# Rotary embedding on one core: six rows of a tile in two groups of three, two rows through TensorE, and declared-away waits

## The chip, the cores and the metric

The kernel runs on one core of a Trainium2 chip. The metric is the device time of one execution in microseconds. The kernel before took 163.06 us, the median of 3 runs (162.94 to 163.31).

## What is computed

x has 16 batches, 512 positions and 1024 channels in float32. The channels of a position are 16 heads of 64. Each head is cut into two halves of 32, x1 and x2, which are rotated by the angle of the position; cos and sin are 512 x 32 and the same for every batch and head.

```python
x = x.reshape(batch, seq, num_heads, head_dim)
x1, x2 = (x[..., :half_dim].copy(), x[..., half_dim:].copy())
rotated = np.concatenate([x1 * cos - x2 * sin, x1 * sin + x2 * cos], axis=-1)
```

So each element needs two products and a sum: x times cos, plus the other half of the head times sin, with a minus for the first half. x is 33.5 MB and the output is 33.5 MB.

## The kernel before, in words

**Tiles.** A tile is two batches: 128 partitions, each with 8 consecutive positions ("rows") of 1024 elements, 32 KB a partition and 4 MB a tile. There are NT = 8 tiles and NB = 5 buffers for x; the result is written over x in the same buffer and stored from there. Tiles 5, 6 and 7 use the buffers of tiles 0, 1 and 2, so their loads wait for the stores of those tiles.

**Tables.** cos and sin lie on 64 partitions and are spread to 128 by products on TensorE with a selecting matrix (L93 to L95). sns holds, per row, -sin for the first half and sin for the second, so one product with it over a view that swaps the halves of each head (`swapped`) gives the second term. sns_ps and cos_ps are the same tables in PSUM; VectorE reads its tables from there, GpSimd reads sns in SBUF.

**Three paths for a row**, all in `compute`:

- Rows 2 to 7 go in PAIRS of two rows. GpSimd makes T = swapped(x) * sns (L131, two T buffers). VectorE makes pp = x * cos in PSUM (L147, one buffer) and then writes x = T + pp (L148).
- Row 0: GpSimd makes B = swapped(x) * sns (L126), VectorE multiplies x by cos in place (L136).
- Row 1: VectorE makes both (L126 and L136).
- For rows 0 and 1 TensorE adds the two in PSUM by products with the identity (L141 with x, L142 with B), in parts of 512 elements, and ScalarE copies each part back into x (L143). ps has two buffers there, one PSUM bank each.

**Order.** The order of the code on each engine is kept as written (`manual_schedule`); the layer below adds the waits that the data and the buffers need. In a tile VectorE does B of row 1, the in-place products of rows 1 and 0, then three times a product and a sum. GpSimd does B of row 0, then three T. A pool's new tile waits until the last reader of the buffer's old tile is done.

**Transfers.** SyncE issues all loads and stores of x and out on one queue, in program order, and waits at each until its condition holds: load 0 in four pieces, loads 1 to 4, stores 0 to 2, loads 5 to 7, stores 3 to 6, store 7 in four pieces. ScalarE issues the two loads of the tables. A store waits for VectorE's sums and for ScalarE's copies of the tile.

Of the kernel before, what the change touches and what calls it, by code (L numbers as in the profile page):

```python
# [7 lines left out]
FP32 = mybir.dt.float32  # L8
ALU = mybir.AluOpType


@with_exitstack
def kernel(
    ctx: ExitStack,
    tc: tile.TileContext,
    x: bass.AP,
    cos: bass.AP,
    sin: bass.AP,
    num_heads: bass.AP,
    out: bass.AP,  # L20
):
    nc = tc.nc
    P = nc.NUM_PARTITIONS
    batch, seq, dim = x.shape
    nh = num_heads
    hd = dim // nh
    half = hd // 2


    BP = 2  # L30
    HP = P // BP
    R = seq // HP
    NT = batch // BP
    assert HP * R == seq and BP * NT == batch
    NB = 5
    PAIRS = (2, 4, 6)
    PEROWS = (0, 1)

    xv = x.rearrange("b (p r) d -> (b p) (r d)", r=R)
    xv = xv.rearrange("(t p) f -> t p f", p=P)  # L40
    ov = out.rearrange("b (p r) h d -> (b p) (r h d)", r=R)
    ov = ov.rearrange("(t p) f -> t p f", p=P)
    cosv = cos.rearrange("(p r) j -> p (r j)", r=R)
    sinv = sin.rearrange("(p r) j -> p (r j)", r=R)

    fixed = ctx.enter_context(tc.tile_pool(name="fixed", bufs=1))
    xin = ctx.enter_context(tc.tile_pool(name="xin", bufs=NB))
    tpool = ctx.enter_context(tc.tile_pool(name="tpool", bufs=2))
    bpool = ctx.enter_context(tc.tile_pool(name="bpool", bufs=2))
    ptab = ctx.enter_context(tc.tile_pool(name="ptab", bufs=1, space=bass.MemoryType.PSUM))  # L50
    ppair = ctx.enter_context(tc.tile_pool(name="ppair", bufs=1, space=bass.MemoryType.PSUM))
    prow = ctx.enter_context(tc.tile_pool(name="prow", bufs=2, space=bass.MemoryType.PSUM))

    ctx.enter_context(tc.manual_schedule())


    x_tiles = [None] * NT
    Q = 2 * dim

    def load(t, pieces=1):  # L60
        x_tiles[t] = xin.tile([P, R * dim], FP32, name="x_sb")
        n = R * dim // pieces
        for i in range(pieces):
            nc.sync.dma_start(out=x_tiles[t][:, i * n:(i + 1) * n], in_=xv[t][:, i * n:(i + 1) * n])

    def store(t, pieces=1):
        n = R * dim // pieces
        for i in range(pieces):
            nc.sync.dma_start(out=ov[t][:, i * n:(i + 1) * n], in_=x_tiles[t][:, i * n:(i + 1) * n])

    load(0, pieces=4)
    tabs = fixed.tile([HP, 2, R * half], FP32, name="tabs")
    nc.scalar.dma_start(out=tabs[:, 1], in_=sinv)
    nc.scalar.dma_start(out=tabs[:, 0], in_=cosv)
    for t in range(1, NB):
        load(t)


    ident = fixed.tile([P, P], FP32, name="ident")
    nc.gpsimd.memset(ident, 0.0)  # L80
    nc.gpsimd.affine_select(  # L81
        out=ident, in_=ident, compare_op=ALU.not_equal, fill=1.0,
        base=0, pattern=[[-1, P]], channel_multiplier=1,
    )
    sel = fixed.tile([HP, 2, P], FP32, name="sel")
    nc.vector.tensor_copy(out=sel[:, 0, :HP], in_=ident[:HP, :HP])  # L86
    nc.vector.tensor_copy(out=sel[:, 0, HP:], in_=ident[:HP, :HP])
    nc.vector.tensor_scalar_mul(out=sel[:, 1, :], in0=sel[:, 0, :], scalar1=-1.0)

    sns_ps = ptab.tile([P, R, 2, half], FP32, name="sns_ps")  # L90
    cos_ps = ptab.tile([P, R, half], FP32, name="cos_ps")
    sin3 = tabs[:, 1].rearrange("p (r j) -> p r j", r=R)
    nc.tensor.matmul(out=sns_ps[:, :, 1, :], lhsT=sel[:, 0, :], rhs=sin3, start=True, stop=True)  # L93
    nc.tensor.matmul(out=sns_ps[:, :, 0, :], lhsT=sel[:, 1, :], rhs=sin3, start=True, stop=True)  # L94
    nc.tensor.matmul(out=cos_ps.rearrange("p r j -> p (r j)"), lhsT=sel[:, 0, :], rhs=tabs[:, 0],  # L95
                     start=True, stop=True)
    sns = fixed.tile([P, R, 2, half], FP32, name="sns")
    cost = fixed.tile([P, R, half], FP32, name="cost")
    nc.scalar.copy(out=sns, in_=sns_ps)  # L99
    nc.scalar.copy(out=cost, in_=cos_ps)  # L100

    def view(ap, r0, n):

        return ap[:, r0 * dim:(r0 + n) * dim]

    def cosb(tab, r0, n):
        return bass.AP(tensor=tab.tensor, offset=tab.offset + r0 * half,
                       ap=[tab.ap[0], [half, n], [0, 2 * nh], [1, half]])

    def snsb(tab, r0, n):  # L110
        return bass.AP(tensor=tab.tensor, offset=tab.offset + r0 * hd,
                       ap=[tab.ap[0], [hd, n], [0, nh], [1, hd]])

    def swapped(xt, r0, n):
        return bass.AP(tensor=xt.tensor, offset=xt.offset + r0 * dim + half,
                       ap=[xt.ap[0], [hd, n * nh], [-half, 2], [1, half]])

    def compute(t):
        xt = x_tiles[t]
        ts = {}  # L120
        bs = {}

        for r in PEROWS:
            B = bpool.tile([P, dim], FP32, name="B")
            eng = nc.vector if r == PEROWS[-1] else nc.gpsimd
            eng.tensor_tensor(out=B, in0=swapped(xt, r, 1), in1=snsb(sns_ps if eng is nc.vector else sns, r, 1),  # L126
                              op=ALU.mult)
            bs[r] = B
        for r0 in PAIRS:
            T = tpool.tile([P, 2 * dim], FP32, name="T")  # L130
            nc.gpsimd.tensor_tensor(out=T, in0=swapped(xt, r0, 2), in1=snsb(sns, r0, 2), op=ALU.mult)  # L131
            ts[r0] = T

        for r in reversed(PEROWS):
            xr = view(xt, r, 1)
            nc.vector.tensor_tensor(out=xr, in0=xr, in1=cosb(cos_ps, r, 1), op=ALU.mult)  # L136
            for c in range(2):
                ps = prow.tile([P, dim // 2], FP32, name="ps")
                xc = xr[:, c * dim // 2:(c + 1) * dim // 2]
                bc = bs[r][:, c * dim // 2:(c + 1) * dim // 2]  # L140
                nc.tensor.matmul(out=ps, lhsT=ident, rhs=xc, start=True, stop=False)  # L141
                nc.tensor.matmul(out=ps, lhsT=ident, rhs=bc, start=False, stop=True)  # L142
                nc.scalar.copy(out=xc, in_=ps)  # L143
        for r0 in PAIRS:
            pp = ppair.tile([P, 2 * dim], FP32, name="pp")
            xr = view(xt, r0, 2)
            nc.vector.tensor_tensor(out=pp, in0=xr, in1=cosb(cos_ps, r0, 2), op=ALU.mult)  # L147
            nc.vector.tensor_tensor(out=xr, in0=ts[r0], in1=pp, op=ALU.add)  # L148

    for t in range(NB):  # L150
        compute(t)
        if t < NT - NB:
            store(t)
    for t in range(NB, NT):
        load(t)
    for t in range(NT - NB, NB):
        store(t)
    for t in range(NB, NT):
        compute(t)
        store(t, pieces=4 if t == NT - 1 else 1)  # L160


# [33 lines left out]
```

## Time and profile before

One execution was taken by the profiler. Its own time is 162.99 us, its span 161.0 us: some 2 us lie around the span.

| what | value |
|---|---|
| runs, median (lowest to highest) | 163.06 us (162.94 to 163.31) |
| profiled execution, its span | 162.99 us, 161.0 us |
| mean granted TensorE clock | 0.758 |
| VectorE's first product, end of its last sum | 8.86 us, 150.60 us |
| a load or store of 4096 KB, issue to landing (median) | 29.5 us, 27.0 us |
| HBM read, written | 33.69 MB, 33.55 MB |

How to read a profile like this one: engines are PE (TensorE's products), PEld (its weight loads), DVE (VectorE), ACT (ScalarE), POOL (GpSimd) and SP (SyncE). A group of instructions is given as line, engine, operation, the tiles it writes and reads, shapes and count; then the busy time in us and the mean ns of one; then the idle time of the engine just before them and what ended it. L131 is line 131 of the kernel before. The rows of busy tenths and of the DMA cut the span into 40 equal slices; 9 is 90% or more. A row of a stretch gives its length, the busy us (and count) of each engine in it, the granted TensorE clock, the DMA share and the GB/s.

### The profile page before, as it was taken

How to read it: one execution, taken by the hardware profiler on the slowest of the kernel's cores; microseconds unless marked ns; L12 is line 12 of the kernel's file. 1: busy time of each engine (PE TensorE's matmuls, PEld its weight loads, DVE VectorE, ACT ScalarE, POOL GpSimd, SP SyncE). 2: the span in 40 equal slices, each digit the busy share in tenths (PEclk: the TensorE clock that was granted, in tenths of full speed). 3: DMA queues.
4: the chain of work that ended last, by engine and by line, in shares of the span. 5: the costliest groups of instructions: out<-in, count | busy, mean ns of one | idle time of the engine just before them, and what ended most of it. 6: DMA issues, size and time to landing. Idle time of an engine off the chain costs nothing. (4 is left out here: it accounts for less than half of the span.)

```text
span 161.0 us, 581 instructions
## 1 busy us (share of the span) xinstructions
PE 78.3 (49%) x134; PEld 32.3 (20%) x134; DVE 137.8 (86%) x75; ACT 21.0 (13%) x35; POOL 127.1 (79%) x38
## 2 busy tenths in 40 slices
PE   0449900598019910894049700990079803991000
PEld 0223300233014400341024200340034202340000
DVE  1077999999999999999999999999999999999400
ACT  3021210014001210022002300121001400121000
POOL 1079999999998799959995999869995999692000
PEclk9999996569755985589957995699655975598555
DMA  5999999999999999999999999999999999999994
GB/s 181 385 419 480 391 497 415 391 472 440 391 456 456 391 432 480 391 415 489 399 417 472 407 415 464 415 407 472 423 399 456 448 399 456 448 391 417 421 423 187
DMA packets 3329, 67.25 MB, mean 418 GB/s; under 512 B 384, under 2 KB 512, under 8 KB 512
## 3 DMA queue, kind: packets, MB, share of 16 engines
q1 hardware_dynamic: 3168, 67.11, 97.6%
q10 hardware_dynamic: 160, 0.13, 0.3%
q14 instruction: 1, 0.01, 0.0%
HBM read 33.69 MB, written 33.55 MB: 418 GB/s over the span
## 5 line engine op out<-in xcount | busy, mean ns | idle before, releaser
L131 POOL TENSOR_TENSOR T<-x_sb,sns 128x2048 f32<-128x2048 f32 x24 | 108.2, 4526 | 10.5 <-DVE x_sb L148 10.5
L141 PE MATMUL ps<-x_sb,ident 128*128 128x512 f32 x64 | 44.8, 790 | 61.0 <-issue 40.4
L148 DVE TENSOR_TENSOR x_sb<-T,pp 128x2048 f32<-128x2048 f32 x24 | 54.9, 2288 | 3.4 <-POOL T L131 1.0
L147 DVE TENSOR_TENSOR pp<-x_sb,cos_ps 128x2048 f32<-128x2048 f32 x24 | 55.0, 2294 | 0.6
L142 PE MATMUL ps<-B,ident 128*128 128x512 f32 x64 | 40.3, 717 | 0.0
L143 ACT COPY x_sb<-ps 128x512 f32<-128x512 f32 x32 | 18.8, 586 | 117.6 <-PE ps L142 117.6
L141 PEld LDWEIGHTS ps<-x_sb,ident 128*128 128x128 f32 x64 | 15.2, 253 | 83.3 <-issue 80.4
L126 POOL TENSOR_TENSOR B<-x_sb,sns 128x1024 f32<-128x1024 f32 x8 | 18.8, 2346 | 7.6 <-ACT sns L99 7.6
L142 PEld LDWEIGHTS ps<-B,ident 128*128 128x128 f32 x64 | 15.4, 241 | 22.0 <-issue 22.0
L136 DVE TENSOR_TENSOR x_sb<-x_sb,cos_ps 128x1024 f32<-128x1024 f32 x16 | 18.8, 1218 | 0.5
L126 DVE TENSOR_TENSOR B<-x_sb,sns_ps 128x1024 f32<-128x1024 f32 x8 | 9.7, 1217 | 7.0 <-ACT sns L99 7.0
L93 PE MATMUL sns_ps<-tabs,sel 64*128 64x256 f32 x2 | 1.2, 697 | 6.2 <-DMA tabs<-in_sin_dram 6.2
L93 PEld LDWEIGHTS sns_ps<-tabs,sel 64*128 64x128 f32 x2 | 0.5, 310 | 6.1 <-issue 6.1
L99 ACT ACT_TABLE_LOAD x1 | 1.3, 1283 | 1.9 <-issue 1.9
L86 DVE COPY sel<-ident 64x64 f32<-64x64 f32 x1 | 0.2, 185 | 1.3 <-POOL ident L81 1.3
L99 ACT COPY sns<-sns_ps 128x512 f32<-128x512 f32 x1 | 0.6, 586 | 5.0 <-PE sns_ps L94 5.0
L95 PE MATMUL cos_ps<-tabs,sel 64*128 64x256 f32 x2 | 1.2, 711 | 0.0
L94 PE MATMUL sns_ps<-tabs,sel 64*128 64x256 f32 x2 | 1.1, 631 | 0.0
L94 PEld LDWEIGHTS sns_ps<-tabs,sel 64*128 64x128 f32 x2 | 0.7, 334 | 0.2
L95 PEld LDWEIGHTS cos_ps<-tabs,sel 64*128 64x128 f32 x2 | 0.5, 306 | 0.6 <-DMA tabs<-in_cos_dram 0.6
L100 ACT COPY cost<-cos_ps 128x256 f32<-128x256 f32 x1 | 0.4, 373 | 0.5 <-PE cos_ps L95 0.5
L80 POOL MEMSET ident<- 128x128 f32 x1 | 0.2, 204 | 0.3 <-POOLq L177 0.3
(7 smaller groups left out, 1.1 us busy)
## 6 DMA issues: line engine op xcount, KB each, us to landing
x_sb<-in_x_dram SPq DMA_DIRECT2D x7, 4096.0 KB, 29.5
out_dram<-x_sb SPq DMA_DIRECT2D x7, 4096.0 KB, 27.0
x_sb<-in_x_dram SPq DMA_DIRECT2D x4, 1024.0 KB, 8.7
out_dram<-x_sb SPq DMA_DIRECT2D x4, 1024.0 KB, 9.2
tabs<-in_sin_dram ACTq DMA_DIRECT2D x1, 64.0 KB, 5.3
tabs<-in_cos_dram ACTq DMA_DIRECT2D x1, 64.0 KB, 6.7
```

What stands on the lines that cost most here:

```text
L93: nc.tensor.matmul(out=sns_ps[:, :, 1, :], lhsT=sel[:, 0, :], rhs=sin3, start=True, stop=True)
L94: nc.tensor.matmul(out=sns_ps[:, :, 0, :], lhsT=sel[:, 1, :], rhs=sin3, start=True, stop=True)
L95: nc.tensor.matmul(out=cos_ps.rearrange("p r j -> p (r j)"), lhsT=sel[:, 0, :], rhs=tabs[:, 0], start=True, stop=True)
L99: nc.scalar.copy(out=sns, in_=sns_ps)
L126: eng.tensor_tensor(out=B, in0=swapped(xt, r, 1), in1=snsb(sns_ps if eng is nc.vector else sns, r, 1), op=ALU.mult)
L131: nc.gpsimd.tensor_tensor(out=T, in0=swapped(xt, r0, 2), in1=snsb(sns, r0, 2), op=ALU.mult)
L136: nc.vector.tensor_tensor(out=xr, in0=xr, in1=cosb(cos_ps, r, 1), op=ALU.mult)
L141: nc.tensor.matmul(out=ps, lhsT=ident, rhs=xc, start=True, stop=False)
L142: nc.tensor.matmul(out=ps, lhsT=ident, rhs=bc, start=False, stop=True)
L143: nc.scalar.copy(out=xc, in_=ps)
L147: nc.vector.tensor_tensor(out=pp, in0=xr, in1=cosb(cos_ps, r0, 2), op=ALU.mult)
L148: nc.vector.tensor_tensor(out=xr, in0=ts[r0], in1=pp, op=ALU.add)
```

## The change

The change gives the 8 rows of a tile another split and writes out which waits are left to others.

- Rows 0 to 2 and 3 to 5 are two groups of three (G, GROUPS): one T, one pp and one sum each, of 3072 elements. Rows 6 and 7 (PEROW) go through TensorE together: one B of 2048 elements on GpSimd, one in-place product a on VectorE, four parts of 512.
- In tile 0 VectorE makes B itself, from sns in SBUF. VectorE has no B in the other tiles.
- PSUM: pp is 3072 elements, so ps has one buffer instead of two. sin's spread table uses ps too; cos_ps stays; sns_ps and the unused copy of cos are gone. sel is written by GpSimd, and ScalarE makes both halves of sns.
- GpSimd's order is T, T in tile 0; T, B, T in tiles 1, 2 and 5 (AFIRST); B, T, T in the others. VectorE begins a tile with a in tiles 1, 2, 5 and 7, and with pp in the others.
- `implied` drops the wait of an instruction for another that an earlier wait of its engine covers; `after` adds a wait. With `after`, VectorE's first product waits for GpSimd's first T in tile 0, a of tiles 3, 4 and 6 waits for the tile's first T, and the second T of tiles 2, 3, 5 and 6 waits for the next tile's load.
- Loads 0 and 1 and stores 5 and 7 are cut at other places.

```diff
-    PAIRS = (2, 4, 6)
-    PEROWS = (0, 1)
+    G = 3
+    GROUPS = (0, 3)
+    PEROW = 6
+    AFIRST = (1, 2, 5)
...
-    ppair = ctx.enter_context(tc.tile_pool(name="ppair", bufs=1, space=bass.MemoryType.PSUM))
-    prow = ctx.enter_context(tc.tile_pool(name="prow", bufs=2, space=bass.MemoryType.PSUM))
+    pgrp = ctx.enter_context(tc.tile_pool(name="pgrp", bufs=1, space=bass.MemoryType.PSUM))
+    prow = ctx.enter_context(tc.tile_pool(name="prow", bufs=1, space=bass.MemoryType.PSUM))
...
+    def implied(inst, *others):
+        for o in others:
+            tc.declare_no_dep(inst.ins, o.ins, reason="implied by an earlier wait of the engine")
...
-    load(0, pieces=4)
+    load(0, (0, 1, 2 * G, 2 * R))
...
+    load(1, (0, 2 * G, 2 * R))
...
-    nc.tensor.matmul(out=sns_ps[:, :, 1, :], lhsT=sel[:, 0, :], rhs=sin3, start=True, stop=True)
-    nc.tensor.matmul(out=sns_ps[:, :, 0, :], lhsT=sel[:, 1, :], rhs=sin3, start=True, stop=True)
+    nc.tensor.matmul(out=sin_ps, lhsT=sel, rhs=tabs[:, 1], start=True, stop=True)
...
-    nc.scalar.copy(out=sns, in_=sns_ps)
-    nc.scalar.copy(out=cost, in_=cos_ps)
+    nc.scalar.copy(out=sns[:, :, 1, :], in_=sin3)
+    nc.scalar.mul(out=sns[:, :, 0, :], in_=sin3, mul=-1.0)
...
+    def second(eng, pool, name, t, r0, n):
+        o = pool.tile([P, n * dim], FP32, name=name)
+        return o, eng.tensor_tensor(out=o, in0=swapped(x_tiles[t], r0, n), in1=snsb(r0, n), op=ALU.mult)
...
+    def pe_rows(t, a):
+        xr = view(x_tiles[t], PEROW, 2)
+        for c in range(4):
+            ps = prow.tile([P, dim // 2], FP32, name="ps")
+            xc = xr[:, c * H:(c + 1) * H]
+            nc.tensor.matmul(out=ps, lhsT=ident, rhs=xc, start=True, stop=False)
+            nc.tensor.matmul(out=ps, lhsT=ident, rhs=Bs[t][:, c * H:(c + 1) * H], start=False, stop=True)
+            i = nc.scalar.copy(out=xc, in_=ps)
...
+        if t == 0:
+            order = (0, 1)
+        elif t in AFIRST:
+            order = (0, "b", 1)
+        else:
+            order = ("b", 0, 1)
...
+        if t == 0:
+            pp, p1 = dve_p(t, 0)
+            after(p1, TIs[t, 0])
+            implied(p1, *loads[t])
+            implied(dve_s(t, 0, pp), *loads[t])
+            Bs[t], b = second(nc.vector, bpool, "B", t, PEROW, 2)
+            a = dve_a(t)
+            pp, p2 = dve_p(t, 1)
+            s2 = dve_s(t, 1, pp)
+        elif t in AFIRST or t == NT - 1:
+            a = dve_a(t)
+            pp, p1 = dve_p(t, 0)
+            s1 = dve_s(t, 0, pp)
+            q, p2 = dve_p(t, 1)
+            s2 = dve_s(t, 1, q)
...
+        else:
+            pp, p1 = dve_p(t, 0)
+            a = dve_a(t)
+            after(a, TIs[t, 0])
+            s1 = dve_s(t, 0, pp)
+            q, p2 = dve_p(t, 1)
+            s2 = dve_s(t, 1, q)
...
-        store(t, pieces=4 if t == NT - 1 else 1)
+        if t == NT - 1:
+            store(t, (0, 2 * G, 4 * G, 2 * R))
+        else:
+            store(t, (0, R, 2 * R) if t == NB else (0, 2 * R))
```

dve_p is pp = x * cos, dve_s the sum T + pp into x, dve_a the in-place product of rows 6 and 7; gp_b and gp_t call `second` on GpSimd. The second T of a tile carries the wait for the next tile's load through a list that is gone through at the end of the program. The instructions that VectorE's order of a tile holds are thus 5 in tiles 1 to 7 and 6 in tile 0.

## The prediction

> **What bounds the kernel now.** I read the table of busy times first, then the DMA row, then the groups of instructions, then the order in time of three tiles, and at last stretches of the span with the granted clock and the DMA rate in each.
>
> ```profile
> PE 78.3 (49%) x134; PEld 32.3 (20%) x134; DVE 137.8 (86%) x75; ACT 21.0 (13%) x35; POOL 127.1 (79%) x38
> ...
> DMA  5999999999999999999999999999999999999994
> ...
> q1 hardware_dynamic: 3168, 67.11, 97.6%
> ...
> L131 POOL TENSOR_TENSOR T<-x_sb,sns 128x2048 f32<-128x2048 f32 x24 | 108.2, 4526 | 10.5 <-DVE x_sb L148 10.5
> ...
> L148 DVE TENSOR_TENSOR x_sb<-T,pp 128x2048 f32<-128x2048 f32 x24 | 54.9, 2288 | 3.4 <-POOL T L131 1.0
> L147 DVE TENSOR_TENSOR pp<-x_sb,cos_ps 128x2048 f32<-128x2048 f32 x24 | 55.0, 2294 | 0.6
> ...
> L126 POOL TENSOR_TENSOR B<-x_sb,sns 128x1024 f32<-128x1024 f32 x8 | 18.8, 2346 | 7.6 <-ACT sns L99 7.6
> ...
> L136 DVE TENSOR_TENSOR x_sb<-x_sb,cos_ps 128x1024 f32<-128x1024 f32 x16 | 18.8, 1218 | 0.5
> ```
>
> The DMA row is full from the second slice to the last but one, and queue q1, which carries x and out, takes 97.6% of the span. VectorE (DVE) is almost as full: it works from 8.86 us to 150.60 with gaps of 0.03 to 0.11. So two chains run side by side, the byte stream and VectorE's loop of 17.55 us a tile (80.11 to 97.66 from B to B). GpSimd (POOL) has slack: 10.5 us of its time goes in waits for a sum to free a T buffer. The stretches show how full the stream is:
>
> ```profile
> 8.00:148.00 140.00, 76.43 (x131) 31.18 (x130) 134.76 (x71) 19.71 (x34) 126.35 (x32) 0.77 1.01 434
> 150.00:158.00 8.00, 0.00 (x0) 0.00 (x0) 0.60 (x1) 0.00 (x0) 0.00 (x0) 0.50 1.01 427
> 158.00:161.00 3.00, 0.00 (x0) 0.00 (x0) 0.00 (x0) 0.00 (x0) 0.00 (x0) 0.50 0.22 93
> ```
>
> The last two numbers of a row are the DMA share and GB/s. The stream moves 434 GB/s in the middle and 427 in the last store. After 158.00 only 0.28 MB moves, 0.65 us of the stream, so bytes end at 158.65 and the span 2.35 later. Since the stream is full, work taken from VectorE cannot bring much; work that comes later than the stream needs it costs its full delay. So I ask when each store becomes ready after the change.
>
> **The parts, with durations.** GpSimd's products run back to back 2.30 us for one row (40.43 to 42.73) and 4.495 for two (8.99 for a pair), so a row more costs 2.195 and three rows 6.69. GpSimd now makes two products of three rows and one of two in each tile: 2 x 6.69 + 4.50 = 17.88 us, where it had 2.30 + 3 x 4.495 = 15.8. VectorE: 1.218 for one row, 2.294 for two, so 1.076 a row and 3.37 for three, with 0.11 from product to sum and 0.03 from sum to product (53.22 + 2.30, next at 55.62; that ends 57.91, next at 57.94). A tile is 2.33 + 2 x 3.48 + 2 x 3.40 = 16.1 us instead of 17.55. **GpSimd becomes the longer of the two**, 17.9 against 16.1, and above the old 17.55.
>
> Waits left out: VectorE's gaps in the loop are 3.5 us in all (3.4 + 0.6 + 0.5 of idle time ahead of its three lines, less 1.0 of waiting for T). A shorter program can save at most that, on an engine that now waits for GpSimd; I cost it at nothing. The instruction queue moved one packet of 0.01 MB, so no fetch shows either.
>
> **Start.** The sin table lands and TensorE starts at 6.17; one product instead of two ends near 7.2 (the second began at 7.15); a copy of 256 elements takes 0.37 (that of cos_ps), the negated one I take alike; GpSimd starts at 8.2, not 8.91. The first three rows of x, 1.57 MB, are there: 2.26 MB had moved by 8.0. Loads and stores are cut elsewhere, but SyncE's queue issues 22 before and after: nothing. VectorE began at 8.86; now its first product waits for GpSimd's first T, 8.2 + 6.69 = 14.9. Behind it stands VectorE's whole program.
>
> **A clash that no row shows.** In tile 0 VectorE makes B from x and sns, both in SBUF; in every loop product and sum of the trace one of its inputs lies in PSUM. GpSimd's T of tile 1 becomes free at the same instant (both wait for the first sum, 21.8). If the two do not disturb each other, as one-SBUF rows do not (a sum is 2.29 beside GpSimd and 2.29 alone at 148.31), the cost is 0. If they exclude each other, either GpSimd waits for VectorE's 2.3 us or VectorE waits for GpSimd's 6.7. I take 2.3, the middle one: after a sum VectorE has started its next instruction at 53.22, 70.78, 88.34 and GpSimd at 53.27, 70.83, 88.39, so VectorE is first by 0.05.
>
> The Trainium skill, SBUF — State Buffer, section "Who interferes with whom", states that a VectorE instruction with two SBUF inputs contends with a GpSimd instruction that reads SBUF. By it the cost would be 2.3 or 6.7 and not 0. No row of this trace shows such a pair.
>
> **The two engines, walked forward.** End times in us; T(t,0) needs the first sum of tile t-1 (two T buffers), T(t,1) the second; a of tiles 1, 2, 5 stands first on VectorE and needs B, which GpSimd makes second there.
>
> | tile | GpSimd, in its order | VectorE a, first sum, second sum |
> |---|---|---|
> | 0 | T 14.9, T 21.6 | first sum 21.8, B 24.1, a 26.4, second 33.3 |
> | 1 | T 30.9, B 35.4, T 42.1 | 37.7, 44.6, 51.5 |
> | 2 | T 51.3, B 55.8, T 62.5 | 58.2, 65.1, 72.0 |
> | 3 | B 67.0, T 73.7, T 80.4 | 77.7, 81.1, 88.0 |
> | 4 | B 84.9, T 91.6, T 98.3 | 93.9, 97.3, 104.2 |
> | 5 | T 105.0, B 109.5, T 116.2 | 111.8, 118.7, 125.6 |
> | 6 | B 120.6, T 127.3, T 134.0 | 131.3, 134.7, 141.6 |
> | 7 | B 138.5, T 145.2, T 151.9 | 143.9, 150.8, 157.7 |
>
> VectorE idles 2.1, 4.4 and 5.3 us ahead of a in tiles 1, 2 and 5 (33.3 to 35.4, 51.5 to 55.9, 104.2 to 109.5). The last sum ends at 157.7 instead of 150.60. Without the clash it is 155.6; with the dearer one 162.4.
>
> **TensorE's rows.** ps has one buffer instead of two, so each of a tile's four 512-wide parts waits for ScalarE's copy of the part before. At half clock a part's copy starts 3.8 after its first pass (117.91, copy at 121.70); with 0.59 for the copy and 0.08 to wake TensorE, a part takes 4.48. At full clock 1.92 (36.16 to 38.08) + 0.67 = 2.6. A tile's four parts took 10.5 from a to the last copy (135.50 to 146.05); now they take between 10.5 (all full) and 17.9 (all half). Which it is depends on the clock:
>
> ```profile
> 117.28:120.69 3.41, 2.78 (x4) 1.26 (x5) 3.41 (x3) 0.00 (x0) 3.41 (x2) 0.50 0.98 423
> 120.69:124.11 3.42, 3.42 (x6) 1.35 (x5) 3.28 (x3) 0.59 (x1) 1.59 (x2) 0.50 1.04 450
> 100.20:103.61 3.41, 3.32 (x4) 1.51 (x5) 3.33 (x2) 0.00 (x0) 3.41 (x1) 0.50 1.07 461
> ```
>
> The matmul passes shorten from 0.85 to 0.43 us at 14.9, 35.4, 52.4, 69.5, 86.6, 103.6, 124.1 and 141.2, all multiples of 3.41 apart. The second and third stretch, busy 100% and 97%, were followed by the full clock; the first, busy 2.78 of 3.41 (81%), was not. In the new rhythm TensorE is busy about 3.5 of every 4.48 us, 79%, so few stretches of 3.41 us are free of a gap. I take three parts at half clock and one at full: 3 x 4.48 + 2.6 + 0.1 = 16.1 us from a to the last copy.
>
> The skill's TensorE: Matmul & The Clock Gate, section "What's actually happening", says the full clock comes after one busy window of about 3.4 us, windows running freely. Read as any busy window it would give one half-clock part, and tile 6 would be ready at 143.5 instead of 147.4; the 81% stretch speaks against that reading.
>
> **Stores, and the sum.** The stream needs tile 6's rows when the stores ahead of it are done: 58.85 MB, of which 2.26 had moved at 8.0, so 8 + 56.6/0.434 = 138.4. They are ready at 131.3 + 16.1 + 0.1 = 147.5, set by TensorE's rows (a is the old in-place product), with the second sum at 141.6 hidden beneath. Data follows an issue by 1.6 (issued 0.73; 0.71 MB moved by 4.0, which is 1.7 us of stream). So store 6 runs from 149.1, and its 4.19 MB and tile 7's 4.19 take 19.65 at 427 GB/s: 168.8. Tile 7's pieces come in time behind it (issued 150.9, 157.8 and, with a at 143.9 + 16.1, 160.1). Plus 2.35: span 171.1. The profiled run took 162.99 for a span of 161.0, so plus 2.0: **173.1 us**. That execution stands 0.07 below the median of the runs, 163.06, so I use the same for both.
>
> Earlier holes don't add. Store 2 is ready at 74.3, 3 us after the stream ran dry, but the stream then catches up by tile 6, whose rows are late in any case. Loads 5 to 7 still land by about 117, before GpSimd and VectorE need them (98.3, 116.2, 134.0; load 5 lands at 96.5, the tightest).
>
> Bounds of this case: parts all at full clock leave the last sum as the bound, 157.8 + 1.6 + 2.62 MB/0.427 = 165.5, time 169.9; all half, 174.9.
>
> **Rivals.**
> 1. No clash in tile 0. All from tile 1 on is 2.1 earlier: 171.0, between 167.8 and 172.8.
> 2. GpSimd takes the clash first: VectorE waits 6.7, the last sum is at 162.4, store 6 goes out at 152.2: 177.8, between 174.5 and 179.5.
> 3. Faster: the stream stays full. VectorE's lighter tile (16.1) would then only feed it earlier, and it would close the dip of the old tail (283 GB/s from 148 to 150): 8 + 64.99/0.434 = 157.7, + 2.35 + 2.0 = 162.0. It decides if tile 6 is ready by 136.8 and the last sum by 150.1 (a 1.6 us lead on the stream). For it: with no waits at all GpSimd ends at 8.2 + 16 x 6.69 + 7 x 4.5 = 146.7 and the last sum 3.4 later, just at that point. Against it: even without a clash the walk has GpSimd waiting 2.5 for tile 1's first sum and VectorE waiting for B in tiles 2 and 5, which puts the last sum at 155.6; and TensorE's rows would have to run at full clock with a shorter gap than the one buffer leaves.
> 4. The same: between 3 and 1, the delays just swallowed by the dip.
>
> That the program is not what the change says can be left out: as built, VectorE has 41 data instructions where the page counts 75, and TensorE and GpSimd hold what the diff says.
>
> **Chances.** Forecast 0.42, rival 1 0.25, rival 2 0.25, rival 3 0.04, rival 4 0.04. So faster by over 0.2% (about what a measurement of this kernel can tell from no change) 0.04, within it 0.04, slower 0.92. Range 167.8 to 179.5, the ends of the three slower cases.
>
> **What would show it.** Right: GpSimd busy near 140 us with T near 6.7; VectorE idle ahead of a in tiles 1, 2 and 5; a longer first T of tile 1 or B of tile 0 (the clash); ScalarE's copies 4.5 us apart in most parts; the DMA row below 9 near 140 to 149. Wrong: a T under 6.2, TensorE mostly at full clock, or a DMA row full to the end.

## The result

The changed kernel takes **168.82 us** (median of 6 executions, 166.42 to 169.87), the kernel before 163.03 in the same comparison (6 executions, 162.69 to 163.31). The ratio is 1.0317, with an interval of 1.0249 to 1.0385: slower by some 3%. Here and below a ratio leaves out executions over 1.5% above the fastest of their kernel, while medians and ranges are over all. The profiled execution took 168.72 us, its span is 166.2, so 2.5 lie around the span.

The executions stand in two groups. Together with a second series of the unaltered changed kernel (experiment 10) there are five between 166.28 and 166.60 and six between 168.72 and 169.87.

### The profile after

The page of the changed kernel, the lines that answer to those shown of before:

```profile
PE 84.7 (51%) x132; PEld 27.6 (17%) x132; DVE 127.0 (76%) x41; ACT 20.7 (12%) x35; POOL 140.9 (85%) x30
...
DMA  5999999899999999939988999999999989799995
...
q1 hardware_dynamic: 3168, 67.11, 95.7%
...
L132 POOL TENSOR_TENSOR T<-x_sb,sns 128x3072 f32<-128x3072 f32 x16 | 108.9, 6826 | 8.8 <-DMA x_sb<-in_x_dram 6.1
...
L142 DVE TENSOR_TENSOR pp<-x_sb,cos_ps 128x3072 f32<-128x3072 f32 x16 | 53.8, 3359 | 14.8 <-POOL T L132 14.4
L146 DVE TENSOR_TENSOR x_sb<-T,pp 128x3072 f32<-128x3072 f32 x16 | 53.6, 3353 | 1.1
...
L132 POOL TENSOR_TENSOR B<-x_sb,sns 128x2048 f32<-128x2048 f32 x7 | 31.7, 4524 | 0.0
L150 DVE TENSOR_TENSOR x_sb<-x_sb,cos_ps 128x2048 f32<-128x2048 f32 x8 | 18.3, 2285 | 12.6 <-POOL B L132 11.9
```

VectorE did become lighter (127.0 us instead of 137.8) and GpSimd heavier (140.9 instead of 127.1). The DMA row, full before, has holes now: a deep one in the slice at 71 to 75 us (the 3), shallow ones after it and near the end. VectorE's waits say who made it late; the columns are the total, the number of waits and the longest, in us:

```profile
DVE pp L142 <- POOL T L132: 14.4, 1, 14.4
DVE x_sb L150 <- POOL B L132: 11.9, 3, 5.4
DVE x_sb L150 <- POOL T L132: 0.7, 1, 0.7
```

After the start VectorE waits 12.6 us in four places. Three are a of tiles 1, 2 and 5, which stands first on VectorE and needs the B that GpSimd makes second. Its last sum ends at 155.43 instead of 150.60.

Where did the stream lose its time? In the table, the bytes moved (summed from the stretches) are set against a stream that goes on from 8.0 us at 434 GB/s, as in the prediction; a value is how many us the stream is behind at that time. The kernels below it are the experiments that carry the argument; all are profiled executions.

| kernel | 62 | 80 | 138 | 144 | 157 | store 2 out, load 5 issued | tile 6's last copy ends | last sum ends | span |
|---|---|---|---|---|---|---|---|---|---|
| before | -0.3 | -0.1 | 0.5 | 0.4 | 0.9 | 63.2 | 128.7 | 150.6 | 161.0 |
| changed | -0.4 | 3.1 | 5.0 | 5.6 | 6.2 | 73.5 | 143.8 | 155.4 | 166.2 |
| changed again (10) | -0.2 | 0.8 | 2.7 | 4.4 | 4.6 | 71.3 | 142.0 | 155.6 | 164.0 |
| order undone (1) | -0.4 | -0.3 | 0.7 | 0.9 | 1.3 | 67.5 | 138.5 | 152.0 | 162.0 |
| no clash (2) | -0.4 | -0.3 | 0.7 | 5.5 | 6.1 | 69.2 | 143.7 | 153.5 | 165.5 |
| no rows (3) | -0.2 | 0.0 | 2.4 | 2.1 | 4.5 | 71.0 | none | 155.2 | 163.7 |
| row 7 shared, a early (11) | -0.2 | -0.2 | 0.7 | 0.6 | 1.7 | 67.5 | 136.5 | 152.5 | 161.4 |

The changed kernel loses 3.5 us between 62 and 80, because store 2 is late and loads 5 to 7 stand behind it on SyncE's queue; by 138 it is 5.0 behind. At 144 tile 6's rows come 0.6 late on top of that. The stretches of the changed kernel at tile 2's store, GB/s last:

```profile
64.00:68.00 4.00, 3.33 (x5) 0.95 (x4) 3.90 (x2) 0.59 (x1) 4.00 (x2) 0.50 1.16 500
68.00:74.00 6.00, 3.78 (x7) 0.90 (x5) 5.96 (x3) 1.17 (x2) 6.00 (x2) 0.83 0.53 229
74.00:78.00 4.00, 1.76 (x3) 0.83 (x4) 4.00 (x2) 0.00 (x0) 4.00 (x1) 0.87 1.04 442
```

At 229 instead of 434 GB/s, 6 us lose 2.8. The granted clock in the first row is 0.50: tile 2's rows run at half clock, their last copy ends at 73.08, and SyncE issues load 5 at 73.54. VectorE had been done with the tile at 70.55. ScalarE's copies of tile 6 show the same rhythm (start, duration, then what ended the idle time):

```profile
133.43 0.59 ACT L160 COPY x_sb<-ps 128x512 f32<-128x512 f32 x1 [11.04 <-PE ps L159]
137.88 0.59 ACT L160 COPY x_sb<-ps 128x512 f32<-128x512 f32 x1 [3.87 <-PE ps L159]
140.54 0.59 ACT L160 COPY x_sb<-ps 128x512 f32<-128x512 f32 x1 [2.07 <-PE ps L159]
143.20 0.59 ACT L160 COPY x_sb<-ps 128x512 f32<-128x512 f32 x1 [2.07 <-PE ps L159]
```

They are 4.45 apart at half clock and 2.66 at full. The clash of tile 0 stands in GpSimd's order in time:

```profile
21.33 8.63 POOL L132 TENSOR_TENSOR T<-x_sb,sns 128x3072 f32<-128x3072 f32 x1 [0.27 <-DVE x_sb L146]
29.91 4.54 POOL L132 TENSOR_TENSOR B<-x_sb,sns 128x2048 f32<-128x2048 f32 x1
34.40 6.71 POOL L132 TENSOR_TENSOR T<-x_sb,sns 128x3072 f32<-128x3072 f32 x1
```

The T that begins at 21.33, beside VectorE's B (21.11 to 23.39), takes 8.63 where the next takes 6.71: 1.92 us more.

### The profile page after: what moved, and what is told of

Read it like the earlier page. It is cut to its first block, busy times and chain, and to the rows that moved or that the text cites. A ratio compares the mean times of both kernels' runs of the same rounds, so it can differ in the third digit from the quotient of the medians.

```text
span 166.2 us, 488 instructions
## 1 busy us (share of the span) xinstructions
PE 84.7 (51%) x132; PEld 27.6 (17%) x132; DVE 127.0 (76%) x41; ACT 20.7 (12%) x35; POOL 140.9 (85%) x30
## 4 chain that ended last, share of the span: by engine, by line
POOL 42%; DVE 36%; issue 10%; DMA 4%; SPq 0%; POOLq 0%; DVEq 0%
POOL T L132 33%; DVE pp L142 16%; DVE x_sb L146 15%; POOL B L132 10%; DVE x_sb L150 5%; DMA x_sb<-in_x_dram 4%; SPq L74 0%; POOLq L132 0%; DVEq L146 0%
## 5 line engine op out<-in xcount | busy, mean ns | idle before, releaser
L132 POOL TENSOR_TENSOR T<-x_sb,sns 128x3072 f32<-128x3072 f32 x16 | 108.9, 6826 | 8.8 <-DMA x_sb<-in_x_dram 6.1
L142 DVE TENSOR_TENSOR pp<-x_sb,cos_ps 128x3072 f32<-128x3072 f32 x16 | 53.8, 3359 | 14.8 <-POOL T L132 14.4
L146 DVE TENSOR_TENSOR x_sb<-T,pp 128x3072 f32<-128x3072 f32 x16 | 53.6, 3353 | 1.1
L159 PE MATMUL ps<-B,ident 128*128 128x512 f32 x64 | 42.8, 759 | 0.0
L132 POOL TENSOR_TENSOR B<-x_sb,sns 128x2048 f32<-128x2048 f32 x7 | 31.7, 4524 | 0.0
L150 DVE TENSOR_TENSOR x_sb<-x_sb,cos_ps 128x2048 f32<-128x2048 f32 x8 | 18.3, 2285 | 12.6 <-POOL B L132 11.9
L158 PEld LDWEIGHTS ps<-x_sb,ident 128*128 128x128 f32 x64 | 11.3, 222 | 95.5 <-issue 47.9
L103 PE MATMUL ps<-tabs,sel 64*128 64x256 f32 x2 | 1.2, 696 | 4.4 <-DMA tabs<-in_sin_dram 4.4
L132 DVE TENSOR_TENSOR B<-x_sb,sns 128x2048 f32<-128x2048 f32 x1 | 2.3, 2284 | 0.0
L103 PEld LDWEIGHTS ps<-tabs,sel 64*128 64x128 f32 x2 | 0.5, 306 | 4.4 <-issue 4.4
```

The costliest lines, as they stand in the source:

```text
L103: nc.tensor.matmul(out=sin_ps, lhsT=sel, rhs=tabs[:, 1], start=True, stop=True)
L132: return o, eng.tensor_tensor(out=o, in0=swapped(x_tiles[t], r0, n), in1=snsb(r0, n), op=ALU.mult)
L142: i = nc.vector.tensor_tensor(out=pp, in0=view(x_tiles[t], GROUPS[g], G), in1=cosb(GROUPS[g], G), op=ALU.mult)
L146: return nc.vector.tensor_tensor(out=view(x_tiles[t], GROUPS[g], G), in0=Ts[t, g], in1=pp, op=ALU.add)
L150: return nc.vector.tensor_tensor(out=xr, in0=xr, in1=cosb(PEROW, 2), op=ALU.mult)
L159: nc.tensor.matmul(out=ps, lhsT=ident, rhs=Bs[t][:, c * H:(c + 1) * H], start=False, stop=True)
```

## The experiments

**The theory:** VectorE's order in tiles 1, 2 and 5 and the clash make a late; rows at a pace of 4.45 and 2.66 us a part, from one ps buffer, make the stores of tiles 2 and 6 later still; the left-out waits matter little. **The rivals:** the lateness comes from the clash alone; or from the one ps buffer alone; or GpSimd's heavier share is simply too much in any order; or the end is set by the last sum, whatever the rows do. Experiments 1 to 4 ran on one chip, 5 to 8 on a second and 9 to 11 on a third, each beside runs of the kernel before (medians 163.23, 163.13 and 163.02).

**1. The order undone.** Tiles 1, 2 and 5 take the order of tiles 3, 4 and 6; the waits that the change leaves out are left in there.

```diff
-    AFIRST = (1, 2, 5)
+    LATE = (1, 2, 5)
...
-        elif t in AFIRST:
-            order = (0, "b", 1)
...
-        elif t in AFIRST or t == NT - 1:
+        elif t == NT - 1:
...
-            for i in (a, p1, s1, p2, s2):
+            for i in () if t in LATE else (a, p1, s1, p2, s2):
```

> The changed kernel with one thing undone: in tiles 1, 2 and 5 VectorE begins with its product and GpSimd with B, as in tiles 3, 4 and 6; the few waits that this order needs are left in. Main theory: the loss is lateness handed down through VectorE's waits for B (2.0, 4.5 and 5.4 us ahead of a in the changed kernel's trace) to the last sum and, through a, to TensorE's rows of tile 6. Those three gaps go, the last sum ends near 151.8 instead of 155.4, and the time falls to about 165, between 163.5 and 168 with the half-clock parts of tile 6. Rival, GpSimd's load alone is the bound whatever the order: the last sum moves by under 1 us and the time stays at 168 to 169. Rival, one ps buffer is the bound: tile 6's last copy stays within 1 us of 143.8, and the time too.

Measured: 165.00 us (163.42 to 166.42, 10 executions), ratio 1.0052 [1.0018, 1.0086]. The profiled execution took 163.87, its stream is full to the end, and the last sum ends at 151.98. VectorE's waits and two lines of GpSimd's order in time in this kernel:

```profile
DVE pp L142 <- POOL T L132: 14.5, 1, 14.5
DVE x_sb L150 <- POOL T L132: 9.0, 5, 2.0
```

```profile
23.64 4.53 POOL L132 TENSOR_TENSOR B<-x_sb,sns 128x2048 f32<-128x2048 f32 x1 [2.51 <-DMA x_sb<-in_x_dram]
28.11 13.38 POOL L132 TENSOR_TENSOR T<-x_sb,sns 128x3072 f32<-128x3072 f32 x2
```

The long waits for B are gone, in their place stand five shorter ones for T, and most of the lost time went with them. Not in every execution, though: the ten stand in two groups, five from 163.42 to 164.22 (the profiled one is of these) and five from 165.78 to 166.42. And the second view shows that this edit isn't as clean as it looked: with B first, GpSimd waits for the load of B's rows until 23.64, when VectorE's product with two SBUF inputs is over. The two T after it take 13.38, 6.69 each. So undoing the order takes the clash away too. Experiments 2 and 6 tell the two apart.

**2. The clash alone taken away.** Tile 0's B on VectorE reads its table from PSUM, in the free half of the bank of cos_ps.

```diff
+    sns67 = bank[:, R * half:R * half + 2 * hd].rearrange("p (r s j) -> p r s j", r=2, s=2)
...
+    nc.scalar.copy(out=sns67, in_=sns[:, PEROW:PEROW + 2])
...
-            Bs[t], b = second(nc.vector, bpool, "B", t, PEROW, 2)
+            Bs[t], b = second(nc.vector, bpool, "B", t, PEROW, 2, snsp(2))
```

> The changed kernel, with VectorE's B of tile 0 reading its table from the free half of the PSUM bank of cos (ScalarE copies the table of rows 6 and 7 there), so that it has one input in SBUF. If two SBUF inputs and a reading GpSimd product exclude each other, GpSimd's first T of tile 1, 8.63 us in the changed kernel, falls to 6.7 and all behind it comes 1.9 earlier: last sum 153.5, time about 167, 1.9 less. If the long T has another cause, it stays at 8.6 and so does the time.

Measured: 166.97 us (165.84 to 167.70, 4 executions), ratio 1.0206 [1.0163, 1.0249]. GpSimd's T falls to its usual time:

```profile
21.39 6.70 POOL L138 TENSOR_TENSOR T<-x_sb,sns 128x3072 f32<-128x3072 f32 x1 [0.27 <-DVE x_sb L152]
```

The last sum ends at 153.53, 1.9 earlier. In time the gain is less clear: the four executions reach from just below the changed kernel's lower group to 1 us below its upper one. In the profiled one (167.70) the rows ran at half clock for longer: tile 6's copies start at 131.52, 135.97, 140.43 and 143.08, three parts at half clock, so that the last ends at 143.67, no earlier than in the changed kernel.

```profile
138.00:144.00 6.00, 4.65 (x8) 1.29 (x7) 5.89 (x3) 1.17 (x2) 6.00 (x2) 0.79 0.19 82
144.00:150.00 6.00, 4.65 (x10) 1.56 (x10) 5.97 (x2) 1.17 (x2) 4.46 (x1) 1.00 1.02 437
```

Here the stream had no hole at tile 2, so it ran dry ahead of tile 6 (82 GB/s), and it starts again the moment the rows are there. From the last copy to the end of the span it takes 165.5 - 143.67 = 21.8 us: 8.39 MB at 427 GB/s are 19.65, and 2.2 remain. With the hole at tile 2 (changed kernel) the span ends only 0.7 later. **In these two executions the two holes don't add.**

**3. No rows on TensorE and ScalarE.** The kernel leaves out TensorE's products and ScalarE's copies, so that rows 6 and 7 hold x times cos only.

```diff
-        pe_rows(t, a)
```

> The changed kernel without TensorE's products with the identity and ScalarE's copies of rows 6 and 7; these rows hold x times cos only, and stores wait for VectorE alone. Main theory: two chains end within 1 us of each other, tile 6's rows and the last sum, so taking one away leaves the other: the last sum stays at 155.4, the hole in the stream near 72 us shrinks from 3 to under 1 us, tile 6's store goes out at 139.8, and the time falls only to 166.5 to 167.5. Rival, one ps buffer is the whole loss: the time falls to 163 to 164. Rival, TensorE's rows don't matter: the same 168.7.

Measured: 165.60 us (165.48 to 165.61, 4 executions), ratio 1.0143 [1.0125, 1.0162], about 1 us below what was expected: a miss. The two groups are gone: the spread is 0.13 us. So the rows make most of the spread of the changed kernel, and some 0.8 to 3 us of its time (166.4 to 168.7 against 165.6). What is left is the last sum:

```profile
151.89 3.35 DVE L146 TENSOR_TENSOR x_sb<-T,pp 128x3072 f32<-128x3072 f32 x1
```

It ends at 155.24; the 2.62 MB that wait for it take 6.14 at 427 GB/s; the span ends 2.3 after that, at 163.7. The rival "the end is set by the last sum" is thus a bound that lies just below, not the whole.

**4. The kernel before with one ps buffer.**

```diff
-    prow = ctx.enter_context(tc.tile_pool(name="prow", bufs=2, space=bass.MemoryType.PSUM))
+    prow = ctx.enter_context(tc.tile_pool(name="prow", bufs=1, space=bass.MemoryType.PSUM))
```

> The kernel before with one ps buffer instead of two, nothing else. TensorE's four parts of a tile then take 10.7 to 17.9 us and not 10.5. In the kernel before the first a is ready 15 us ahead of the tile's last sum, so the rows still end within 3 us of it. Main theory: the time rises by 0 to 1.5 us, to 163.0 to 164.5, since the single buffer costs only where a comes late. Rival, the single buffer costs by itself: 166 or more.

Measured: 163.38 us (162.67 to 165.81, 10 executions), ratio 1.0006 [0.9984, 1.0027]. Nine of the ten lie between 162.67 and 163.96, about where the kernel before lies (162.77 to 163.83): one buffer costs nothing there, so it isn't the cause by itself. The one traced execution is the slowest, 165.81; in it tile 7's copies start 4.45 us apart twice, and the stream stands at 33 GB/s from 148 to 152. A changed kernel with two ps buffers wasn't run: the change gave up the second one for the larger pp. Experiment 11 has one buffer and keeps the stream full.

**5. The waits left in.**

```diff
-            tc.declare_no_dep(inst.ins, o.ins, reason="implied by an earlier wait of the engine")
+            pass
```

> The changed kernel with no wait declared away: the function that drops implied waits does nothing; the order, the groups and the added waits are as in the changed kernel. Main theory: the left-out waits are worth almost nothing here, since VectorE waits for GpSimd in several tiles; the gaps of VectorE grow by a few hundredths of a us each, the last sum stays within 0.7 us of 155.4 and the time within 166.5 to 170, like the changed kernel's own runs (166.4 to 169.9). Rival, the shorter program is worth something by itself: the time rises by 1 us or more over those, to 170 and above.

Measured: 167.84 us (166.85 to 168.88, 4 executions), ratio 1.0295 [1.0246, 1.0344], within the changed kernel's own range. The left-out waits show in one place only, the last sum:

```profile
152.34 3.35 DVE L146 TENSOR_TENSOR x_sb<-T,pp 128x3072 f32<-128x3072 f32 x1 [0.53 <-DVE pp L142]
```

It begins 0.53 us after the product's end, in the changed kernel 0.10. The page of this kernel counts one packet on a second instruction queue (q14), which that of the changed kernel doesn't. So in these two executions leaving the waits out is worth about 0.4 us at the last sum; that it changes the time isn't shown. Nor is the packet shown to be the cause: the pages of kernels 7 and 11 count such a packet too, and no gap of more than 0.2 us stands in VectorE's order in time there after the start.

**6. Order and clash undone together** (the edits of 1 and 2).

> The changed kernel with the order of e1_order (product first in tiles 1, 2 and 5) and the table of e2_noclash (tile 0's B with one input in SBUF) together. Main theory: what the two take away adds up as far as the stream allows. The last sum ends near 150.1, tile 6's last copy between 135 and 142 by the clock, and the time lies between 162.5 and 165, the kernel before at its lower end, because the stream of 67 MB is then full again but for the half-clock parts. Rival, order and clash hide each other: no better than e1_order, 165.

Measured: 164.48 us (163.40 to 166.72, 10 executions), ratio 1.0051 [1.0029, 1.0073]; last sum at 151.89, against 151.98 with the order alone. The expected gain of the second edit isn't there: as experiment 1 showed, there is no clash left to remove. GpSimd again waits 2.52 us for the load ahead of tile 1's B. Against experiment 1 the rival held: no better.

Against experiment 2, which has no clash either, this kernel differs in the order alone. The order by itself is thus worth 1.6 us at the last sum (153.53 to 151.89) and brings the ratio from 1.0206 to 1.0051; the two intervals lie apart.

**7. Row 7's B on VectorE** as well (with 6): GpSimd's B has one row, as in the kernel before. Of the edit, against the changed kernel:

```diff
-        Bs[t], TIs[t, "b"] = second(nc.gpsimd, bpool, "B", t, PEROW, 2)
+        o = bpool.tile([P, 2 * dim], FP32, name="B")
+        Bs[t] = o
+        TIs[t, "b"] = nc.gpsimd.tensor_tensor(out=o[:, :dim], in0=swapped(x_tiles[t], PEROW, 1), in1=snsb(PEROW, 1), op=ALU.mult)
...
+    def dve_b7(t):
+        tab = bass.AP(tensor=sns67.tensor, offset=sns67.offset + hd, ap=[sns67.ap[0], [hd, 1], [0, nh], [1, hd]])
+        nc.vector.tensor_tensor(out=Bs[t][:, dim:], in0=swapped(x_tiles[t], PEROW + 1, 1), in1=tab, op=ALU.mult)
...
+            dve_b7(t)
             pp, p1 = dve_p(t, 0)
```

> As e7_order_noclash, and in tiles 1 to 7 the B of row 7 is made by VectorE from the PSUM table, as the kernel before did for its row 1. GpSimd then has 2 x 6.7 + 2.3 = 15.7 us a tile and VectorE 15.9 + 1.25 = 17.1. If GpSimd's load is what still costs after the order and the clash, the time falls below e7_order_noclash, to 162.0 to 163.5. By the main theory the stream is the bound by then, so it is within 1 us of e7_order_noclash, 162.5 to 165, with the last sum near 151.

Measured: 164.74 us (163.09 to 166.31, 12 executions), ratio 1.0058 [1.0026, 1.0090]. VectorE waits nowhere after the start and the last sum is at 149.81, 2.1 earlier than in 6, but the time is not better. A heavy GpSimd by itself is therefore not what keeps these kernels above 163. In the profiled execution, which is a quick one, the stream is full; what makes the others up to 3 us longer this run doesn't show, and experiment 11 takes it up.

**8. Tile 0 begins with B and a** on VectorE (with 6), in place of waiting for GpSimd's first T. The edit in tile 0, against the changed kernel:

```diff
+            Bs[t], b = second(nc.vector, bpool, "B", t, PEROW, 2, snsp(2))
+            a = dve_a(t)
             pp, p1 = dve_p(t, 0)
-            after(p1, TIs[t, 0])
-            implied(p1, *loads[t])
-            implied(dve_s(t, 0, pp), *loads[t])
-            Bs[t], b = second(nc.vector, bpool, "B", t, PEROW, 2)
-            a = dve_a(t)
+            dve_s(t, 0, pp)
             pp, p2 = dve_p(t, 1)
             s2 = dve_s(t, 1, pp)
```

> As e7_order_noclash, and in tile 0 VectorE begins with B and a, which need no T, so that it no longer waits for GpSimd's first T at 14.4. Main theory: VectorE's start moves from 14.4 to about 10 and TensorE's first rows from 26 to 15, but GpSimd, which was not waiting there, keeps its times, so the last sum moves by under 0.5 us (from about 150) and the time stays within 1 us of e7_order_noclash. Rival, VectorE's late start still sets the end: 2 us or more are gained, to below the kernel before.

Measured: 163.61 us (163.08 to 166.73, 12 executions), ratio 1.0028 [1.0008, 1.0048]. The time is as expected, but VectorE's start moved little, to 13.9 and not to 10: it now waits for the piece of x that holds rows 6 and 7, instead of 14.5 us for T. The last sum ends at 152.03.

**9. The tail of the kernel before:** tile 7's four store pieces issued in the order 1, 0, 2, 3, so that the piece that waits for the copies isn't ahead of one that is ready.

```diff
-        for i in range(pieces):
+        for i in (1, 0, 2, 3) if pieces == 4 else range(pieces):
```

> The kernel before with the four pieces of tile 7's store issued in the order rows 2 and 3, rows 0 and 1, rows 4 and 5, rows 6 and 7. Before, rows 2 and 3 (done at 141.2) stand in SyncE's queue behind rows 0 and 1 (ScalarE's last copy at 146.05), and the stream dips to 283 GB/s between 148 and 150, which is 0.7 us of stream. If the stream is the bound of the kernel before, the dip closes and the time falls by 0.3 to 0.7, to 162.4 to 162.8. If VectorE's chain is, nothing changes.

Measured: 163.19 us (162.85 to 163.48, 12 executions), ratio 1.0004 [0.9991, 1.0017]: a miss. The dip of the tail stays (307 GB/s from 148 to 150, 283 before), after a stretch of 492 (524 before). A stretch of 2 us probably reads the same bytes once too early and once too late; that is argued only. By the expectation's words no change would also fit VectorE's chain as the bound of the kernel before. Experiment 11 speaks against that: its last sum ends 1.9 us later than in the kernel before (152.51, 150.60), and the time is 0.3 us longer.

**10. The changed kernel once more,** unaltered, for its spread.

> The changed kernel once more, unaltered, for its spread. Main theory: VectorE's and GpSimd's times repeat to 0.3 us (last sum at 155.1 to 155.7 in the profile), and the span less 22.1 us is the end of ScalarE's last copy of tile 6 where that comes after 143.5, else the span is 163.7 to 164.2, set by the last sum. So times lie between 165.6 and 170. If times vary with VectorE's last sum instead, the theory of the two chains falls.

Measured: 166.32 us (166.28 to 168.82, 5 executions), ratio 1.0201 [1.0179, 1.0223]. The profiled execution (166.60) is one of the lower group, and shows what tells it from the one of 168.72. Tile 6's copies in it:

```profile
133.42 0.59 ACT L160 COPY x_sb<-ps 128x512 f32<-128x512 f32 x1 [12.15 <-PE ps L159]
136.08 0.59 ACT L160 COPY x_sb<-ps 128x512 f32<-128x512 f32 x1 [2.07 <-PE ps L159]
...
141.40 0.59 ACT L160 COPY x_sb<-ps 128x512 f32<-128x512 f32 x1 [2.07 <-PE ps L159]
```

The first copy starts within 0.01 us of the other execution's, and all the rest are 2.66 apart. Tile 2's rows were quick too, so store 2 waited for VectorE alone and load 5 went out at 71.28 instead of 73.54: 2.3 us, and the span is 2.2 shorter. Same program, same waits of VectorE (11.9 us for B in both); only the clock fell otherwise. The rows of tile 6 end at 141.99 here, so the last sum (155.60) is the bound, and the span of 164.0 is the one expected for that case.

**11. Row 7 on VectorE, and a early in every tile:** kernel 7 with B and a ahead of pp (the edit is shown against the changed kernel).

```diff
+            dve_b7(t)
+            a = dve_a(t)
             pp, p1 = dve_p(t, 0)
-            a = dve_a(t)
-            after(a, TIs[t, 0])
             s1 = dve_s(t, 0, pp)
```

> As e8_row7, with a (and row 7's B) first on VectorE in tiles 1 to 6 too. GpSimd's B is now one row and stands first, so a does not wait for it; a and with it TensorE's rows come 3.3 us earlier in a tile than in e8_row7. Main theory: the spread of e8_row7 (163.1 to 166.3) comes from tile 6's rows at half clock arriving after the stream has run dry; with 3.3 us in hand they arrive in time, the spread shrinks to under 1 us and the median is 163.0 to 163.6. Rival, the spread has another cause: it stays, and the median at 164.7.

Measured: 163.35 us (163.04 to 163.49, 12 executions), ratio 1.0016 [1.0004, 1.0028]. Its page and VectorE's waits:

```profile
DMA  5999999999999999999999999999999999999895
```

```profile
DVE pp L150 <- POOL T L138: 14.7, 1, 14.7
```

With a early the rows have time at either clock (two steps of 4.45 us in each of tiles 6 and 7 here), the spread is 0.45 us, and the stream is full again. This is the best of the family with groups of three, and it is not better than the kernel before: both are near the stream's own length. No version tried was faster than the kernel before.

## Why the prediction was right, and where its sum was off

The forecast was slower, 173.1 us in a range of 167.8 to 179.5. The direction and the range held, and so did the chain of delays on GpSimd, VectorE and TensorE; the time came out 4.3 below the forecast. Where the stream lost its time is another matter: mostly at store 2, which the forecast had set aside, and not at store 6, by which it was summed. That the sum came so near is in part luck, since the two losses are of like size and the later one takes up the earlier. By its steps:

- **What bounds the kernel: right.** Before, the stream is full (0.9 behind at 157); what was taken off VectorE (10.8 us of busy time) bought nothing. Kernel 11, with full stream, has a median of 163.35.
- **GpSimd the longer engine: right.** 6.69 and 4.50 predicted, 6.70 (kernel 2) and 4.52 measured; busy 140.9, "near 140".
- **VectorE's idle time ahead of a: right.** 2.1, 4.4 and 5.3 predicted, 11.8 in all; measured 11.9, the longest 5.4. Experiment 1 shows what it costs: undone, together with the clash that goes with it, the last sum is 3.5 us earlier and the ratio falls to 1.0052; experiments 2 and 6 give the order alone 1.6 of the 3.5.
- **The clash: right**, with the middle bound: 2.3 taken, 1.92 measured, VectorE first. Rival 1 (none) and rival 2 (6.7) fall by the 8.63 us of that T. It is the rule of the Trainium skill, SBUF — State Buffer, section "Who interferes with whom", that the prediction weighed, and here a run shows it: 8.63 beside a product with two SBUF inputs, 6.70 beside one that has its table in PSUM.
- **Start of GpSimd at 8.2:** 7.76. The sin table landed at 4.4, not 6.17, and x's landing set the start instead. With 0.4 from the clash and VectorE's tile at 15.83 us instead of 16.1, a of tile 6 ended at 129.54 instead of 131.3: **-1.8**.
- **TensorE's rows, 16.1 us in tile 6: mis-sized.** The rhythm was right (4.48 and 2.6 predicted, 4.45 and 2.66 measured), but two parts ran at half clock and not three: 14.25, **-1.85**. Kernel 2 had the three, the second series none after the first part. This term isn't one number: it depends on where the clock's windows fall. (With one half-clock part the prediction's own terms give 143.7, not 143.5.)
- **Store 6 to the end:** predicted 23.7 from the last copy (0.1 + 1.6 + 19.65 + 2.35), measured 22.4, and 21.8 in kernel 2: **-1.3**. Both ends of the term were too long. In kernel 2, where the stream stood empty, 0 GB/s from 143 to 144 are followed by 524 from 144 to 145, so data come some 0.3 us behind the last copy (143.67) and not 1.6; and no more than 11 GB/s flow in the last 1.5 us of the span, where 2.35 were taken. The bytes between took about 20.0 us, not 19.65.
- **Around the span:** 2.5, not 2.0: **+0.5**. The four make -4.45, and 173.1 - 4.45 = 168.7, the profiled time.
- **"Earlier holes don't add": right in effect, wrong in its reason.** The prediction let the stream "catch up" by tile 6. It doesn't: it was 3.1 us behind at 80 and 5.0 at 138, and a stream that was full before has nothing to catch up with. Store 2's hole is where this execution lost most (3.5 us by 80; by the prediction's own figures, 70.7 for the dry stream and 74.3 for the store, 3.6 and not 3), and tile 6's rows came only 0.6 late on a stream that was 5.0 behind by then. Kernel 2 had tile 6's hole without the other and ended 0.7 earlier, so that hole alone makes nearly all of the loss; no run has store 2's whole hole alone. Some 1.9 us more trickled away between 80 and 138, also in the second series and in kernel 3, and not in 1, 2 and 11; the cause of that stays open.
- **The last sum as the bound behind the rows: right, mis-sized.** The prediction took it for the case of all parts at full clock, at 169.9. It stands 2.3 below the span of 166.2 (155.43 + 6.14 + 2.3 = 163.9), and is the bound itself where the rows are quick: 155.60 + 8.4 = 164.0, the span of the second series, at 166.60.
- **Waits left out, at nothing: nearly right.** 0.4 us at the last sum, in no comparison of times to be seen (experiment 5).
- **Rival 3 (the stream stays full, 162.0): missed conditions, and a price too low.** The changed kernel missed both of its conditions (tile 6 at 143.8 and not 136.8, last sum at 155.4 and not 150.1). Kernel 7 meets both in its profiled execution (133.2 and 149.8), and that took 163.37: the dip in the old tail that the rival wanted to close gave nothing there, nor in experiment 9. The conditions were stricter than need be, as kernel 11 keeps the stream full with a last sum at 152.5.

## What to carry to other kernels

Where a stream of bytes is full, as here, a lighter engine buys nothing, and the thing to look at is when each store becomes ready: walk the engines forward and compare with when the stream would run dry. Time that such a stream has lost wasn't made up later here. An order that lets one engine begin with what another makes second makes both wait. And a chain through one PSUM buffer should have slack for the half clock, since its pace (here 4.45 or 2.66 us a part) changes from execution to execution.

## What the runs showed of the hardware

- **The clash shows as a longer GpSimd instruction,** not as a later one: it began 0.22 us after VectorE's and took 8.63 instead of 6.70, nearly VectorE's 2.28 more, while VectorE's took its usual time.
- **A busy window need not be a full one to bring the full clock.** Three stretches of the changed kernel (PE's busy time first, the granted clock before the last two columns):

```profile
131.40:134.80 3.40, 2.73 (x4) 0.84 (x3) 3.37 (x2) 0.59 (x1) 3.40 (x2) 0.50 0.96 414
134.80:138.20 3.40, 3.04 (x4) 0.67 (x2) 3.30 (x2) 0.32 (x1) 3.40 (x2) 0.50 1.01 434
138.20:141.60 3.40, 2.40 (x5) 0.98 (x6) 3.40 (x2) 0.85 (x2) 3.40 (x1) 0.98 0.97 414
```

  The first, busy 80%, left the clock at half; the second, 89%, was followed by the full clock, which then held through a stretch busy 71%. These stretches are cut within 0.2 us of the clock's own windows. Cut exactly there, 3.41 us apart from a change of the granted clock on, the twelve traces with rows on TensorE narrow the border to 81%: of the windows at half clock all 58 that were busy over 81.2% were followed by the full clock, and none of the 104 busy under 80.5%. The full clock was lost only after windows busy 41% or less. The rhythm of one ps buffer lies between: some 80% at half clock, just too little to raise it, and 71% at full, enough to keep it. So each pace keeps itself up, until a window falls otherwise. The Trainium skill, TensorE: Matmul & The Clock Gate, section "What's actually happening", puts the full clock behind at least one busy window of some 3.4 us; these traces agree, with busy meaning over 81%.
- **A stream can end late on little traffic.** The traced execution of kernel 8 (166.52 us) had all rows and sums done by 152.1, and its stretches at the end read:

```profile
158.00:160.00 2.00, 0.00 (x0) 0.00 (x0) 0.00 (x0) 0.00 (x0) 0.00 (x0) 0.50 0.86 363
160.00:162.00 2.00, 0.00 (x0) 0.00 (x0) 0.00 (x0) 0.00 (x0) 0.00 (x0) 0.50 0.07 31
```

  427 GB/s over 16 DMA engines are 27 each; 31, and 16 in the next 2 us, would fit one engine that finishes alone, some 3 us behind the others. It is a single execution; why it happened, and whether it is also behind the spread of kernels 1, 6 and 7, whose traced executions are quick ones, stays open.
